# The sample's gathered rows of layer 0, issued without waiting for the first gate span

## The chip, the cores and the metric

The kernel runs on one core of one Trainium2 chip. The metric is the device time of one execution in microseconds (us). Engines are named as in the profile: PE is TensorE (PEld its weight loads), DVE is VectorE, ACT is ScalarE, POOL is GpSimd, SP is SyncE, whose queue issues the plain loads and stores.

## What is computed

One inference step of a two-layer encoder for two groups that share all weights: a prompt of 512 frames (four blocks of 128, B0 to B3) and a sample S of 64 frames. Each layer mixes (attention, mLSTM, chunk MLP) and then adds an expert layer:

```python
def layer(x, ...):
    x = x + concat([o_da, o_ml, o_cm]) @ w_out
    xn2 = rmsnorm(x, norm2_g)
    x = x + peer(xn2, peer_wq, peer_keys, peer_u, peer_v)

def peer(x, w_q, keys, u_tab, v_tab):            # per frame
    s = q(x) . keys                              # 8 heads, two halves of 128 keys
    e, g = top 16 of the 256 sums of two top-16 lists, softmax of their scores
    act = gelu(u_tab[e] . x)                     # 8 x 16 rows of 1024 of 16384
    return sum((g * act) * v_tab[e])
```

## The kernel before

The expert layer is done in two ways. For two blocks of each layer it is dense: all 16384 experts are multiplied on PE in 128 chunks, and a gate matrix W, zero except at the chosen experts, weights them. In layer 0 these are B0 and B1, in layer 1 B2 and B3. For the other two blocks and S only the chosen rows are fetched (gathered). A gather is one indirect DMA of POOL that fetches one row of 1024 float32 for each of 128 partitions (512 KB).

`gather_u` (L971) prepares the normalized frames: a sum of squares on ACT that uses the tile `xn` for its junk output (L236), a chain of small DVE operations for the inverse root (L226 to L231), and the scaled `xn` on DVE (L976). Then, for each of `npair` columns (128, for S 64, because S puts four heads on each half of the partitions), it gathers a row of `peer_u` (L960) and takes its dot product with `xn` on DVE (L984, and an accumulator read behind it). After each 32 of them ACT takes the GELU of 32 values (L987), and DVE multiplies them by the softmax weights (L988). `gather_v` (L992) gathers the rows of `peer_v` and adds each, times its factor, to x on DVE (L996). For S two small DMAs on the SP queue belong to it: L978 copies `xn` to the upper 64 partitions, and L1001 brings the upper half sum back. Rows come into six buffers (`row` 4, `row2` 2), and there is one `xn`.

One layer runs as a list of steps. For layer 0 the order is `N1 P1 N2 Q1 M1+P2 O1+Q2 S1+M2 F1+O2 S2`: N, P and Q are norm and projections, M the mixing, O the output projection (L396), S the scores and the top-16 selection (PE at L407 and L830, DVE at L912 to L953), F the end of the selection. Group 1 is B0, B1 and S; group 2 is B2 and B3. The selection of S is done early, inside S1, in two halves of 32 columns (the indices are written at L904). Then comes the first gate span (`first_gate`, 32 batches: DVE at L1020 to L1024, PE at L1028, ACT at L1030), woven with the first 12 chunks of the dense part (L1058), and the dense part itself (PE at L1058 and L1098, gate products on DVE at L1091, gelu on ACT at L1067). In layer 1 the order is `N1 P1 Q1 M1+R O1 S1 N2 P2 F1+Q2 M2 O2`, then S2 and the dense part; R is B3's `peer_v` rows of layer 0, spread over M1.

All instructions of an engine run in an order that is fixed when the program is built. A list scheduler goes through a model of time: whenever an engine is free in it, it takes the ready instruction with the most urgent priority. `low` (L1004) gives the gathers a very late priority, so that they are taken only when nothing else of that engine is ready, but an instruction once started is not broken off. `behind` adds an order to this without a semaphore: the later instruction must stand behind the earlier one on its engine. In layer 0 `gather_u` is called with `after=self.gated`, the last DVE instruction of the first gate span, so that the `xn` of each gathered group, and with it all its dot products, stands behind that span. In layer 1 there is no such order. The gathers of layer 0 go in the order S, B2, B3; B3's `peer_v` rows follow in layer 1 as R.

Of the kernel before, what the change touches and what calls it, by code (L numbers as in the profile page):

```python
# [92 lines left out]
def weave(*streams):  # L93
    live = [[g, n, 0] for g, n in streams]
    while live:
        r = min(live, key=lambda r: r[2] / r[1])
        r[2] += 1
        try:
            next(r[0])
        except StopIteration:  # L100
            live.remove(r)


def run(gen):
    for _ in gen:
        pass
# [14 lines left out]
class Build:  # L121
# [994 lines left out]
    def run(self):  # L1116
        tc = self.tc
        self.S = Tok("s", NS, None)
        self.B = [Tok(f"b{i}", P, i) for i in range(4)]
        self.setup()  # L1120
        S, B = self.S, self.B
        g1, g2 = [B[0], B[1], S], [B[2], B[3]]
        for t in [S] + B:
            t.npair = 64 if t.sample else P
            t.c0 = TD if t.sample else (t.blk % 2) * P
        for l in range(DEPTH):
            D = g2 if l else g1[:2]
            for i, t in enumerate([S] + B):
                t.dense, t.order, t.early = t in D, i, t.sample
            self.sel = self.ca.tile([P, TD // 8, 4, 8], F16, tag="sel", name="sel")  # L1130
            self.select_pool()
            with ExitStack() as es:
                self.mixer_pools(es.enter_context, l)
                L = self.layer_params(l)
                steps = {
                    "N1": lambda: [(self.norm_in(l, L, g1), 1)], "N2": lambda: [(self.norm_in(l, L, g2), 1)],
                    "P1": lambda: [(self.project_a(l, L, g1), 4)], "Q1": lambda: [(self.project_b(l, L, g1), 2)],
                    "P2": lambda: [(self.project_a(l, L, g2), 4)], "Q2": lambda: [(self.project_b(l, L, g2), 2)],
                    "M1": lambda: self.mix(l, L, g1), "M2": lambda: self.mix(l, L, g2),
                    "O1": lambda: [(self.out_proj(l, g1), 2)], "O2": lambda: [(self.out_proj(l, g2), 2)],  # L1140
                    "S1": lambda: [(self.scores(l, L, g1), 18)], "S2": lambda: [(self.scores(l, L, g2), 18)], "F1": lambda: [(self.finish_select(l, g1), 3)],
                    "R": lambda: [(self.rest_v(B[3], REST_STEP), REST_PARTS)]}
                for part in ORDER[l].split():
                    weave(*[s for k in part.split("+") for s in steps[k]()])
                if l == 0:
                    self.low(lambda: run(self.finish_select(l, g2)), by=MID)
            with ExitStack() as es:
                self.dense_pools(es.enter_context, l)
                nlead = LAG[l] + 8 * PRE[l]
                if l == 0:  # L1150
                    xT = self.split(self.dx.tile([P, KC, TD], F32, tag="xTd", name="xTd"))
                    self.norm_T(D, Q_G2, L, xT)
                    dense = self.peer_dense(l, D, xT)
                    weave((self.first_gate(l), 32), (itertools.islice(dense, nlead), nlead))
                else:
                    sc = self.scores(l, L, g2)
                    next(sc)
                    dense = self.peer_dense(l, D, self.xT2)
                    weave((itertools.islice(dense, EARLY_LEADS), EARLY_LEADS), (sc, 18))
                    run(itertools.islice(dense, nlead - EARLY_LEADS))  # L1160
                    run(self.finish_select(l, g2))
                    self.close_scores(es.enter_context, l)
                    run(self.first_gate(l))
                run(dense)
            for t in [S] + B:
                if not t.dense:
                    self.low(self.gather_u, l, L, t, None if l else self.gated)
                    if l or t is not B[3]:
                        self.low(self.gather_v, t, 0, P)
        self.fg = self.lp.tile([P, R_N], F32, tag="row", name="fg")[:, :DM]  # L1170
        self.nc.sync.dma_start(self.fg, self.bcast_rows(self.h["final_g"], DM))
        for t in [S] + B:
            self.final(t)
# [91 lines left out]
```

## Time and profile before

| quantity | value |
|---|---|
| median of 3 runs | 3612.36 us (3599.8 to 3621.32) |
| profiled execution | 3629.34 us, span 3627.6 us |
| PE busy | 3095.5 us (85%) |
| DVE busy | 2563.4 us (71%) |
| POOL busy | 1565.4 us (43%) |
| ACT busy | 670.5 us (18%) |
| DMA | 1060.20 MB, mean 292 GB/s |

Busy time is a sum over the whole span, whose stages have different limits, so stages are read one by one: the table by windows gives for each stretch the time for which each engine was busy, the TensorE clock that was granted (as a share of full speed), and the share and rate of the 16 DMA engines.

### The profile page before, as it was taken

The numbers are of one execution on the slowest core, as the hardware profiler recorded it, in microseconds if no ns is written. First come the engines' busy times: TensorE is split into PE (matmuls) and PEld (weight loads), VectorE is DVE, ScalarE is ACT, GpSimd is POOL, SyncE is SP. The second block draws the span as 40 slices with busy tenths as digits, with TensorE's granted clock in tenths as the row PEclk, the third lists the DMA queues.
The fourth block names the chain that finished last, engine by engine and source line by source line (L and its number), as shares of the span: only waits on it lengthen the run. The fifth ranks groups of instructions, "written<-read, shape, count | busy, mean of one in ns | idle before, by whom it ended". The sixth has DMA issues, their size and how long they took to land.

```text
span 3627.6 us, 41388 instructions
## 1 busy us (share of the span) xinstructions
PE 3095.5 (85%) x13384; PEld 2076.9 (57%) x13384; DVE 2563.4 (71%) x5915; ACT 670.5 (18%) x2589; POOL 1565.4 (43%) x1284
## 2 busy tenths in 40 slices
PE   8989877789999999985977896567566999999998
PEld 6767646646666666652543654245453566666655
DVE  4554677776687666666688898879998768766611
ACT  4444222400121000001222222111131002100000
POOL 0000000076545445455557335655667665666600
PEclk9999989899999999997978997688877999999999
DMA  5332322299999999998879687999888999999954
GB/s 180 100 101 76 98 90 82 85 354 403 374 343 398 409 407 407 409 396 324 327 216 351 238 317 278 288 335 332 323 303 293 408 407 361 382 402 400 398 172 122
DMA packets 299928, 1060.20 MB, mean 292 GB/s; under 512 B 36372, under 2 KB 39232, under 8 KB 299712
## 3 DMA queue, kind: packets, MB, share of 16 engines
q0 software_dynamic: 184320, 671.17, 49.7%
q1 hardware_dynamic: 115392, 386.38, 29.7%
q8 instruction: 107, 1.75, 0.2%
q14 instruction: 109, 0.89, 0.1%
HBM read 1048.09 MB, written 8.27 MB: 291 GB/s over the span
## 4 chain that ended last, share of the span: by engine, by line
PE 42%; DVE 17%; DMA 16%; issue 13%; POOL 7%; another core or an unknown queue 2%; ACT 2%; SPq 0%; POOLq 0%; DVEq 0%; ACTq 0%
PE y L1098 12%; PE H L1058 11%; DMA row<-in_peer_v_dram,idx 9%; POOL row L960 7%; PE ps L396 7%; PE ps L407 5%; DVE row L984 5%; DMA row<-in_peer_u_dram,idx 3%; DVE x_b L996 2%; DMA V<-in_peer_v_dram 2%; PE ps L572 1%; PE ps L1028 1%; PE ps L574 1%; DVE i L913 1%
## 5 line engine op out<-in xcount | busy, mean ns | idle before, releaser
L960 POOL DMA_INDIRECT row<-in_peer_u_dram,idx x640 | 773.2, 1208 | 1358.1 <-DVE row L984 670.4
L960 POOL DMA_INDIRECT row<-in_peer_v_dram,idx x640 | 792.0, 1238 | 522.4 <-DVE x_b L996 262.2
L984 DVE SCALAR_TENSOR_TENSOR row<-row,xn 128x1024 f32<-128x1024 f32 x640 | 773.1, 1222 | 156.1 <-DMA row<-in_peer_u_dram,idx 149.4
L1098 PE MATMUL y<-V,A 128*128 128x512 f32 x1856 | 835.1, 598 | 25.4 <-DMA V<-in_peer_v_dram 18.0
L996 DVE SCALAR_TENSOR_TENSOR x_b<-row,hb,x_b 128x1024 f32<-128x1024 f32 x512 | 656.4, 1282 | 148.8 <-DMA row<-in_peer_v_dram,idx 138.3
L1098 PEld LDWEIGHTS y<-V,A 128*128 128x128 f32 x1856 | 352.5, 192 | 403.0 <-issue 371.9
L1058 PE MATMUL H<-xT,U 128*128 128x256 f32 x2048 | 485.6, 391 | 55.3 <-ACT pre L1067 24.4
L1058 PE MATMUL H<-xTd,U 128*128 128x256 f32 x2048 | 470.1, 383 | 12.0 <-ACT A L1067 10.0
L1058 PEld LDWEIGHTS H<-xT,U 128*128 128x128 f32 x2048 | 393.6, 195 | 149.4 <-issue 35.0
L1058 PEld LDWEIGHTS H<-xTd,U 128*128 128x128 f32 x2048 | 388.0, 191 | 105.8 <-issue 41.0
L407 PE MATMUL ps<-xT,w 128*128 128x320 f32 (+1 forms) x1280 | 343.4, 424 | 33.6 <-DMA w<-in_wt_dram 22.5
L1067 ACT ACTIVATE A<-H 128x256 f32<-128x256 f32 x232 | 89.1, 384 | 1388.2 <-PE H L1058 770.6
L1091 DVE TENSOR_TENSOR A<-A,W 128x256 f32<-128x256 f32 x232 | 97.1, 423 | 333.7 <-ACT A L1067 330.1
L407 PEld LDWEIGHTS ps<-xT,w 128*128 128x128 f32 x1280 | 248.8, 199 | 103.7 <-issue 15.1
L1030 ACT ACTIVATE W<-ps 128x64 f32<-128x64 f32 x1024 | 137.5, 321 | 260.7 <-PE ps L1028 151.9
L996 DVE SCALAR_TENSOR_TENSOR x_s<-row,hb,x_s 128x1024 f32<-128x1024 f32 x128 | 164.1, 1282 | 21.5 <-DMA row<-in_peer_v_dram,idx 19.5
L396 PE MATMUL ps<-w,xT 128*128 128x512 f32 (+3 forms) x320 | 133.1, 567 | 22.1 <-DMA w<-in_wn_dram 15.8
L1028 PE MATMUL ps<-o,o 128*128 128x64 f16 x2048 | 87.4, 200 | 73.9 <-DVE o L1024 73.7
L1028 PEld LDWEIGHTS <-o 128*128 128x128 f16 x2048 | 81.2, 103 | 106.5 <-issue 50.4
L1098 PE MATMUL y<-V,pre 128*128 128x512 f32 x192 | 100.6, 681 | 24.6 <-DMA V<-in_peer_v_dram 21.7
L351 DVE TENSOR_TENSOR wl<-w,wh 128x1024 fp32r<-128x1024 f32 (+1 forms) x56 | 64.4, 1150 | 76.3 <-PE ps L396 56.5
L1020 DVE TENSOR_TENSOR o<-jj,sel 128x1024 f16<-128x1024 f16 x128 | 87.9, 688 | 41.2 <-PE ps L1028 39.8
(314 smaller groups left out, 3049.3 us busy)
## 6 DMA issues: line engine op xcount, KB each, us to landing
V<-in_peer_v_dram SPq DMA_DIRECT2D x256, 512.0 KB
U<-in_uT_dram SPq DMA_DIRECT2D x256, 512.0 KB
w<-in_wt_dram SPq DMA_DIRECT2D x96, 512.0 KB
w<-in_wn_dram SPq DMA_DIRECT2D x80, 512.0 KB
row<-in_peer_u_dram,idx POOLq DMA_INDIRECT x640
row<-in_peer_v_dram,idx POOLq DMA_INDIRECT x640
w<-in_keysT_dram SPq DMA_DIRECT2D x16, 256.0 KB
w<-in_wn_dram SPq DMA_DIRECT2D x8, 264.0 KB
```

The costliest lines, as they stand in the source:

```text
L396: self.nc.tensor.matmul(p[:t.n, :wd], x[kk][:, t.c0:t.c0 + t.n], ww[:, k * wd:(k + 1) * wd], start=(kk + part + j == 0), stop=(kk == KC - ...
L407: self.nc.tensor.matmul(ps, ww[:, k * P:(k + 1) * P], x[k][:, :n], start=(k + part + j == 0), stop=(k == KC - 1 and part == pair and j == ...
L960: self.nc.gpsimd.indirect_dma_start(out=row, out_offset=None, in_=self.h[tab], in_offset=bass.IndirectOffsetOnAxis(ap=t.idx[:, k:k + 1], a ...
L984: nc.vector.scalar_tensor_tensor(row, row, 1.0, xn, op0=ALU.mult, op1=ALU.mult, accum_out=hb[:, k:k + 1])
L996: op = nc.vector.scalar_tensor_tensor(x, row, t.hb[:, k:k + 1], x, op0=ALU.mult, op1=ALU.add)
L1020: nc.vector.tensor_tensor(o2, self.jj[:, None].to_broadcast([P, 4, P, 2]), sel[:, 1, :, None, :].to_broadcast([P, 4, P, 2]), op=ALU.is_equal)
L1028: nc.tensor.matmul(pb[:, j, :nq], o2[:, j // 2, :, j % 2], o1[:, p, j // 2, :, j % 2], start=(p == 0), stop=(p == 1))
L1030: nc.scalar.activation(W[:, :, t0:t0 + 8].rearrange("p i t -> p t i"), pb[:, :, 8 * i:8 * i + 8], AF.Copy, scale=1.0 / GSCALE)
L1058: mm = nc.tensor.matmul(hp, U[:, k, :], xT[k], start=(k == 0), stop=(k == KC - 1))
L1067: nc.scalar.activation(a, hp, AF.Gelu)
L1091: gated = nc.vector.tensor_tensor(a, a, Ws[ci // 8][:, ci % 8, :], op=ALU.mult)
L1098: nc.tensor.matmul(ys[i][:, hf, :], a[:, i * P:(i + 1) * P], V[:, hf * 512:(hf + 1) * 512], start=(c == 0), stop=(c == NCH - 1))
```

## The change

The order behind the first gate span is left out for S in layer 0. B2 and B3 keep it. Nothing else is edited.

```diff
             for t in [S] + B:
                 if not t.dense:
-                    self.low(self.gather_u, l, L, t, None if l else self.gated)
+                    self.low(self.gather_u, l, L, t, None if l or t.sample else self.gated)
                     if l or t is not B[3]:
                         self.low(self.gather_v, t, 0, P)
```

## Rows read from the trace of the kernel before

**Rows 1.** Page, section 5: group of instructions, busy us, mean ns, idle before it.

```profile
L996 DVE SCALAR_TENSOR_TENSOR x_s<-row,hb,x_s 128x1024 f32<-128x1024 f32 x128 | 164.1, 1282 | 21.5 <-DMA row<-in_peer_v_dram,idx 19.5
```

**Rows 2.** Timeline of POOL: start, duration, instruction, idle time before and releaser.

```profile
408.77 1.07 POOL L960 DMA_INDIRECT row<-in_peer_u_dram,idx  x1 [408.31 <-DVE on L609]
...
731.09 6.27 POOL L960 DMA_INDIRECT row<-in_peer_u_dram,idx  x1 [315.03 <-DVE row L984]
```

**Rows 3.** Timeline of DVE: S's second indices, its scaled frames, its first dot product.

```profile
491.54 0.19 DVE L904 SCALAR_TENSOR_TENSOR idx<-es 128x32 int32<-128x32 f32 x1
...
720.63 1.27 DVE L976 SCALAR_TENSOR_TENSOR xn<-x_s,rs_y,row 64x1024 f32<-64x1024 f32 x1
...
729.60 1.21 DVE L984 SCALAR_TENSOR_TENSOR row<-row,xn 128x1024 f32<-128x1024 f32 x1
```

**Rows 4.** Windows of layer 0: stretch, length, busy us (instructions) by engine, clock, DMA.

```profile
core 0: us, PE busy (x) PEld busy (x) DVE busy (x) ACT busy (x) POOL busy (x), PEclk, DMA share, GB/s
408.00:490.00 82.00, 54.77 (x238) 36.86 (x236) 60.16 (x362) 19.74 (x76) 5.76 (x6) 0.83 0.38 110
490.00:522.00 32.00, 26.39 (x62) 11.89 (x62) 25.05 (x63) 6.74 (x16) 0.00 (x0) 0.87 0.39 123
522.00:612.00 90.00, 80.82 (x420) 71.40 (x421) 53.43 (x336) 21.89 (x84) 0.00 (x0) 0.95 0.30 91
612.00:648.00 36.00, 6.96 (x47) 6.26 (x46) 35.49 (x162) 4.86 (x18) 0.00 (x0) 0.65 0.05 15
648.00:722.00 74.00, 67.90 (x736) 59.88 (x735) 50.74 (x97) 38.34 (x266) 0.00 (x0) 0.94 0.35 101
```

**Rows 5.** The same windows for S2 and the end of selection in layer 1.

```profile
2407.00:2550.00 143.00, 105.85 (x498) 89.77 (x498) 128.53 (x467) 22.92 (x81) 83.50 (x72) 0.88 0.94 340
2550.00:2648.00 98.00, 56.90 (x202) 44.56 (x202) 94.51 (x269) 12.98 (x28) 66.07 (x51) 0.79 0.92 335
```

**Rows 6.** Windows of L984 alone (DVE): second stretch of rows 5.

```profile
2550.00:2648.00 98.00, 56.18 (x92) 0.79 0.92 335
```

**Rows 7.** Line L984 within 2407 to 2550: idle before it, and who waited for it.

```profile
  DMA row<-in_peer_u_dram,idx: 13.7, 10
...
  ACT hb L987: 36.2, 2
```

**Rows 8.** Line L830, idle of PE before it (us, times): 522 to 612, then 2407 to 2550.

```profile
  ACT pq L824: 5.8, 8
...
  ACT pq L824: 50.9, 18
```

**Rows 9.** Timeline of DVE in the end of selection in layer 1.

```profile
2626.65 1.21 DVE L984 SCALAR_TENSOR_TENSOR row<-row,xn 128x1024 f32<-128x1024 f32 x1
...
2627.79 0.28 DVE L894 TENSOR_TENSOR sel<-gr,sel 128x128 f16<-128x128 f32 x1
2628.00 1.21 DVE L984 SCALAR_TENSOR_TENSOR row<-row,xn 128x1024 f32<-128x1024 f32 x1
```

**Rows 10.** Windows of the dense part of layer 0, its end, and the start of layer 1.

```profile
729.00:1636.00 907.00, 863.59 (x3339) 555.28 (x3337) 636.73 (x928) 85.00 (x384) 498.51 (x436) 0.98 1.00 391
1550.00:1600.00 50.00, 47.51 (x163) 31.23 (x163) 33.40 (x65) 5.30 (x10) 28.17 (x25) 0.97 1.01 396
1600.00:1636.00 36.00, 26.75 (x65) 12.50 (x63) 24.72 (x43) 0.77 (x2) 21.30 (x19) 0.91 1.01 393
1636.00:1706.00 70.00, 28.29 (x86) 14.95 (x86) 57.12 (x110) 11.02 (x34) 50.52 (x46) 0.70 0.98 365
1706.00:1794.00 88.00, 86.20 (x249) 42.05 (x248) 40.75 (x84) 16.26 (x34) 42.05 (x30) 0.97 0.77 279
```

**Rows 11.** Timelines at the start of layer 1: DVE's root chain (first and last), PE.

```profile
1646.97 0.17 DVE L226 TENSOR_SCALAR rs_v<-ssn 128x3 f32<-128x3 f32 x1
...
1656.67 0.16 DVE L231 SCALAR_TENSOR_TENSOR rs_y<-rs_t,rs_y 128x3 f32<-128x3 f32 x1
...
1705.29 10.46 PE L396 MATMUL ps<-w,xT 128*128 128x512 f32 x16 [14.47 <-DMA w<-in_wn_dram]
```

## The prediction

> **What bounds the kernel now.** I read the table by windows first, because the change moves work between stages with different limits. In the dense part of layer 0, 729 to 1636 us, PE is busy 863.6 of 907 us while the DMA share is 1.00 and DVE is busy only 636.7 us [rows 10]. The reader is to see that PE sets the end there, and that 436 gathers are served beside it at almost no cost. In the mixer that goes before, 408 to 722 us, the DMA share is 0.05 to 0.39 [rows 4]: this is where the change puts the sample's gathers. But DVE is far from idle: 21.8 + 7.0 + 36.6 + 0.5 + 23.3 = 89.2 us are free in 314. Who sets the pace changes from stretch to stretch. In 522 to 612 (the scores) PE is busy 80.8 of 90 us; in 612 to 648 (the end of the selection) DVE is busy 35.5 of 36 and PE 7.0.
>
> The timelines of POOL and DVE come next. Six gathers of the sample are issued from 408.8 us on, as many as there are row buffers; the next one waits 315.0 us for a dot product [rows 2]. The scaled frames come at 720.6 us among the last operations of the gate span, and the first dot product at 729.6 [rows 3]. So the order that the change removes does bind. Without it the sample's first 32 columns can run from about 410 us, the other 32 from 491.5, when their indices are written [rows 3], then the 64 of `peer_v`.
>
> **What moves.** The sample has 64 dot products and 64 additions. A dot product costs DVE 1.22 us (56.18 us for 46 with their accumulator reads [rows 6]), an addition 1.28 [rows 1]: 78 + 82 = 160 us of DVE, and 122 gathers of 512 KB (six are early already). One scaling (1.27 us [rows 3]), two small GELUs on ACT, and the two SP copies L978 and L1001 move with them. POOL carries nothing but gathers, so nothing queues behind them there. On SP weight loads stand behind the two copies, and on ACT the evacuations of PE's results stand behind the GELUs; that is in the cost below.
>
> **What it costs before the gate.** If all 128 are done before the gate span ends, DVE needs 160 us and has 89.2: at least 71 us longer, if DVE binds. If only idle time is filled, 0. No reason allows less than 0, as work is only added there. The nearest rows are the same stages in layer 1, which run with gathers at the same late priority and without the order.
>
> First, 408 to 490: 32 dot products, 39 us, against 21.8 free; between 0 and 17, I take 10.
>
> Second, 490 to 612: in layer 1, 72 gathers were issued in the 143 us of the scores [rows 5], 0.5 per us. By that rate about 66 fit in these 122 us and the time that they add. PE's idle time in the scores grew from 9.2 us (90 - 80.8 [rows 4]) to 37.2 (143 - 105.9 [rows 5]), thus 28 us or 0.39 us per gather. How it comes is in the rows: ACT's GELU of the factors waited 36.2 us for dot products [rows 7], and PE waited 50.9 us for ACT's evacuation, against 5.8 in layer 0 [rows 8]. 13.7 us of DVE's waits there were for rows under a DMA share of 0.94 [rows 5, 7], which the mixer of layer 0 does not have. So 0.2 to 0.39 each, 13 to 26 us; I take 20.
>
> Third, 612 to 648: the remaining 30. Here the pattern is plain. In layer 1 a dot product stands between almost every two selection operations [rows 9], since the later one is not ready at the moment at which the earlier one ends in the scheduler's model, and a late priority loses only to what is ready. DVE's own work in that stage is about equal in both layers (94.5 - 56.2 = 38 us with a few additions in it; 35.5 in layer 0), yet it took 98 us with 51 gathers and 36 without [rows 4 to 6]: 1.2 us each. 30 x 1.2 = 36 us, between 0 and 36.
>
> The gate span of 74 us is then left with no sample work: 0. Sum: 10 + 20 + 36 = 66 us, bounds 0 and 95. The upper one is 17 + 26 + 36, and 16 for the copies on SP and the GELU's waits, which a mean from layer 1 may miss.
>
> **What it gives back.** The dense part then starts on B2 at once. B2 and B3 have 128 + 128 + 128 gathers left, against 436 served before [rows 10], so B3's `peer_u` rows end some 50 gathers before the dense part does, and the 76 that now run in 1636 to 1794 (46 and 30 [rows 10]) are gone. That B3's `peer_v` rows could use the room is excluded: they are tied to M1 of layer 1. The gains are three. The end of the dense part: PE lost 2.5 us in 1550 to 1600 and 9.2 in 1600 to 1636 [rows 10]; I take 9 of 11.7. The start of layer 1: 70 us in 1636 to 1706 with PE busy 28.3, at 0.70 of the clock, because the root chain took 9.9 us with dot products between its small steps and PE then waited 14.5 us for a weight load under a DMA share of 0.98 [rows 10, 11]. The chain alone is 11 steps of under 0.2 us, so 7.6 us are sure; with the load and the low clock I take 25, at most 42 (70 - 28.3). The rest to 1794: PE is busy 86.2 of 88, so at most 1.8, taken as 2. Sum: 36 us, bounds 15 and 55.
>
> A page speaks for more. The Trainium skill, Perfetto Trace Analysis, section Optimization Strategy, says that a kernel whose most-contended engine changes over time may gain by interleaving the regimes. The DMA shares of 0.3 and 1.00 look like such a pair; what it would give here is the first rival. The trace agrees only in part, since the engine with slack in the dense part is DVE, and DVE is what the selection lacks.
>
> **Forecast.** 66 - 36 = +30 us. Against the profile's own execution of 3629.34 that is 3659; it lies 17 us above the median of 3612.36, so the median to expect is 3642 us.
>
> **Rivals.**
> First, faster: the list scheduler puts sample rows only where DVE is idle. Then 89.2 / 1.25 = 71 columns move, nearly the 76 that layer 1 gets rid of, and the rest stays behind the gate. Cost about 5, gain 36: -31, 3581 us. It decides in 612 to 648: if under 5 sample rows stand among the selection, this is what happened. For it: PE sets the pace in 490 to 612, where DVE has 43.6 us free [rows 4]. Against it: the dense row of insertions in layer 1 [rows 9].
> Second, no change: the insertions cost about what the start of layer 1 gives back, for example 10 instead of 30 in the end of the selection (66 - 24 = 42 against 36): +6, 3618 us. Here belongs also that the change does nothing, because something else holds the sample's scaled frames; against that, x of the sample is final after O1, before the scores that gave the indices of the gathers at 408.8 us [rows 2], so that only the order is left.
> Third, worse: each GELU holds ACT as long as in layer 1 (36.2 us for two [rows 7]) and PE with it, and DVE has no free slot: 95 against 25: +70, 3682 us.
>
> **How the numbers follow.** The forecast has a chance of 0.40, the first rival 0.20, the second 0.27, the third 0.13. A measurement of this kernel can tell about 0.5%, 18 us, from no change. So faster 0.20, same 0.27, slower 0.53. For 8 in 10 the range reaches half into the first and the third rival: 3583 to 3682 us. The forecast's own range is 3625 to 3665.
>
> **What the profile would show.** POOL issues the sample's gathers through 410 to 720 us and not from 731; DVE is over 90% busy from 490 to the end of the selection; the gate span (L1028) begins at about 714 instead of 648 us [rows 4]; B3's last dot product stands before the end of the dense part; and the stretch from that end to the first full-speed projection shrinks from 70 to about 45 us. I am wrong in the sign if L1028 comes less than 36 us late, and wrong in the mechanism if DVE shows free time among the selection while the stage is still longer.

## The result, and the profile after

The changed kernel took 3669.82 us (median of four runs, 3662.56 to 3676.45), the kernel before 3616.84 beside it: a ratio of 1.0172, 95% interval 1.0147 to 1.0197, or 53 us more. In a second series, with both kernels run again, it was 3675.81 against 3612.67, 1.0193 (1.0154 to 1.0233). The forecast was 3642 us, 30 more than the median then known.

The stages tell where it went. Each number is the start, in us, of the first or last instruction of a line; the two columns "again" are the profiles of the second series.

| boundary | before | after | before, again | after, again |
|---|---|---|---|---|
| first score product, L830 | 310.6 | 315.2 | 314.7 | 312.9 |
| S's second indices, L904 | 491.5 | 514.6 | 493.8 | 512.2 |
| last score product, L831 | 610.8 | 675.1 | 618.4 | 678.3 |
| first gate product, L1028 | 649.4 | 747.8 | 657.0 | 745.3 |
| end of the dense part, first of the last two L1105 | 1639.7 | 1724.3 | 1648.4 | 1722.4 |
| last first projection of layer 1, L396 | 1769.8 | 1817.3 | 1757.5 | 1816.2 |
| last L1105 | 3612.0 | 3655.2 | 3597.9 | 3658.7 |

From the first score product to the first gate product the kernel before took 338.8 and 342.3 us, the changed one 432.6 and 432.4. Six further kernels below leave this stage as it was before (335 to 341 us), and one that leaves the sample out has 334.2; I call 338 us the stage without sample rows, and the cost is then **94 us**. From there to the last L1105 the changed kernel took 2907.4 and 2913.4 us against 2962.6 and 2940.9: it gets 55 us back by the first pair of profiles and 27.5 by the second. Leaving the sample out gives 32 us in run times (below), so the second pair is nearer to the typical case.

Windows of the profile after, over the stretches of [rows 4] as they now lie (length, busy us and instructions by engine, clock, DMA share, GB/s):

```profile
core 0: us, PE busy (x) PEld busy (x) DVE busy (x) ACT busy (x) POOL busy (x), PEclk, DMA share, GB/s
408.00:490.00 82.00, 51.83 (x222) 34.24 (x223) 76.12 (x301) 17.17 (x63) 38.58 (x32) 0.86 0.76 264
490.00:522.00 32.00, 16.84 (x44) 9.61 (x43) 29.61 (x167) 6.88 (x19) 5.72 (x5) 0.56 0.23 76
522.00:612.00 90.00, 61.79 (x231) 42.24 (x230) 83.36 (x214) 19.30 (x60) 58.37 (x47) 0.83 0.95 354
612.00:680.00 68.00, 55.56 (x274) 47.28 (x273) 67.96 (x240) 14.16 (x55) 36.05 (x33) 0.90 0.91 323
680.00:747.00 67.00, 2.60 (x13) 2.04 (x12) 66.37 (x233) 3.69 (x8) 19.09 (x19) 0.54 0.48 152
```

DVE, busy 60.2 of the first 82 us and 53.4 of the 90 us of the scores before [rows 4], is now full from 408 us to the gate: 323.4 of 339 us. PE no longer sets the pace; in 522 to 612 it is busy 61.8 us instead of 80.8. The DMA share, 0.30 among the scores before, is 0.95.

POOL's timeline shows the sample's gathers where [rows 2] had the wait of 315 us (start, duration, instruction, idle before and releaser). The first gather of the first 32 columns, the first and the last of the other 96, and the first row of B2 stand here:

```profile
413.33 1.08 POOL L960 DMA_INDIRECT row<-in_peer_u_dram,idx  x1 [412.88 <-DVE on L609]
...
515.06 1.68 POOL L960 DMA_INDIRECT row<-in_peer_u_dram,idx  x1 [38.91 <-DVE idx L904]
...
707.38 0.94 POOL L960 DMA_INDIRECT row<-in_peer_v_dram,idx  x1 [1.99 <-DVE cand L914]
737.78 1.68 POOL L960 DMA_INDIRECT row<-in_peer_u_dram,idx  x1 [29.46 <-DVE idx L904]
```

DVE's timeline in the end of the selection has the picture that [rows 9] showed for layer 1, an addition of 1.26 us among operations of 0.1 to 0.3:

```profile
691.49 0.27 DVE L913 FIND_INDEX8 i<-v,s 128x8 uint32<-128x128 f32 x1
691.69 1.25 DVE L996 SCALAR_TENSOR_TENSOR x_s<-row,hb,x_s 128x1024 f32<-128x1024 f32 x1
692.88 0.07 DVE L916 MATCH_VALUE_LOAD ci<-vsel,cand 128x8 f32 x1
...
694.34 0.26 DVE L914 MATCH_REPLACE8 s<-v,s 128x128 f32<-128x128 f32 x1
694.53 1.26 DVE L996 SCALAR_TENSOR_TENSOR x_s<-row,hb,x_s 128x1024 f32<-128x1024 f32 x1
695.72 0.07 DVE L914 MATCH_VALUE_LOAD s<-v,s 128x8 f32 x1
```

Who kept PE waiting between 408 us and the gate, after (engine, line and releaser: us in total, times, longest):

```profile
PE ps L754 <- DVE kn L748: 23.4, 1, 23.4
PE ps L407 <- DMA w<-in_wt_dram: 17.1, 8, 5.6
PE ps L884 <- DVE es L953: 12.6, 2, 10.0
PE ps L214 <- DVE oh L952: 11.3, 1, 11.3
PE ps L830 <- ACT pq L824: 6.1, 10, 1.4
```

The three large single waits, 23.4, 10.0 and 11.3 us, are for DVE: mixing and selection that come late behind sample rows. Waits for weights (`in_wt`) come next, 17.1 us against 7.6 from 408 us to the gate of the kernel before. The wait for a score's evacuation, 50.9 us in layer 1 [rows 8] and the mechanism of the third rival, is 6.1 us.

At the other end B3's last dot product (the last start in the first line, L984) now stands 101 us ahead of the end of the dense part. Where [rows 11] had 9.9 us, the root chain at the start of layer 1 takes 2 us, and full-speed projections begin 20 us after the dense end:

```profile
L984 DVE SCALAR_TENSOR_TENSOR row<-row,xn x128: 1212/1220/1276, 1357.5 to 1622.8; 128x1024 f32<-128x1024 f32 x128
...
1724.30 1.23 DVE L1105 TENSOR_TENSOR x_b<-y,x_b 128x1024 f32<-128x1024 f32 x1 [4.31 <-PE y L1098]
1729.70 0.17 DVE L226 TENSOR_SCALAR rs_v<-ssn 128x3 f32<-128x3 f32 x1 [2.03 <-ACT junk L367]
1731.67 0.16 DVE L231 SCALAR_TENSOR_TENSOR rs_y<-rs_t,rs_y 128x3 f32<-128x3 f32 x1
1744.24 18.98 PE L396 MATMUL ps<-w,xT 128*128 128x512 f32 x42
```

### The profile page after: what moved, and what is told of

It reads as the page before. It is cut to its first block, busy times and chain, and to the rows that moved or that the text cites. A ratio compares the mean times of both kernels' runs of the same rounds, so it can differ in the third digit from the quotient of the medians.

```text
span 3670.8 us, 41380 instructions
## 1 busy us (share of the span) xinstructions
PE 3092.7 (84%) x13384; PEld 2066.4 (56%) x13384; DVE 2539.6 (69%) x5915; ACT 675.5 (18%) x2593; POOL 1614.5 (44%) x1284
## 4 chain that ended last, share of the span: by engine, by line
PE 57%; DVE 21%; issue 10%; DMA 8%; ACT 2%; POOL 2%; SPq 0%; DVEq 0%; POOLq 0%; ACTq 0%
PE y L1098 21%; PE H L1058 19%; PE ps L396 7%; DVE row L984 5%; PE ps L407 3%; DMA row<-in_peer_v_dram,idx 3%; DMA row<-in_peer_u_dram,idx 2%; DVE x_b L996 2%; DMA V<-in_peer_v_dram 2%; DVE x_s L996 2%; POOL row L960 2%; PE ps L1028 1%; PE ps L572 1%; ACT A L1067 1%; DVE i L913 1%
## 5 line engine op out<-in xcount | busy, mean ns | idle before, releaser
L960 POOL DMA_INDIRECT row<-in_peer_u_dram,idx x640 | 781.1, 1221 | 1152.4 <-DVE on L609 412.9
L960 POOL DMA_INDIRECT row<-in_peer_v_dram,idx x640 | 833.2, 1302 | 713.9 <-DVE x_b L996 441.8
L984 DVE SCALAR_TENSOR_TENSOR row<-row,xn 128x1024 f32<-128x1024 f32 x640 | 768.0, 1221 | 91.6 <-DMA row<-in_peer_u_dram,idx 87.4
L1098 PE MATMUL y<-V,A 128*128 128x512 f32 x1856 | 824.3, 595 | 5.3 <-DMA V<-in_peer_v_dram 5.3
L996 DVE SCALAR_TENSOR_TENSOR x_b<-row,hb,x_b 128x1024 f32<-128x1024 f32 x512 | 655.7, 1281 | 69.1 <-DMA row<-in_peer_v_dram,idx 56.9
L1098 PEld LDWEIGHTS y<-V,A 128*128 128x128 f32 x1856 | 352.3, 191 | 393.3 <-issue 380.0
L1091 DVE TENSOR_TENSOR A<-A,W 128x256 f32<-128x256 f32 x232 | 97.2, 424 | 551.8 <-ACT A L1067 551.3
L407 PE MATMUL ps<-xT,w 128*128 128x320 f32 (+1 forms) x1280 | 347.6, 428 | 41.7 <-DMA w<-in_wt_dram 39.3
L407 PEld LDWEIGHTS ps<-xT,w 128*128 128x128 f32 x1280 | 251.5, 201 | 113.8 <-DMA w<-in_wt_dram 38.2
L1028 PE MATMUL ps<-o,o 128*128 128x64 f16 x2048 | 85.7, 201 | 109.7 <-DVE o L1024 109.0
L996 DVE SCALAR_TENSOR_TENSOR x_s<-row,hb,x_s 128x1024 f32<-128x1024 f32 x128 | 163.1, 1274 | 14.0 <-DMA row<-in_peer_v_dram,idx 13.2
L1028 PEld LDWEIGHTS <-o 128*128 128x128 f16 x2048 | 79.8, 103 | 139.2 <-issue 77.1
L396 PE MATMUL ps<-w,xT 128*128 128x512 f32 (+3 forms) x320 | 128.7, 553 | 10.5 <-ACT v L448 7.1
L1098 PE MATMUL y<-V,pre 128*128 128x512 f32 x192 | 101.2, 683 | 34.7 <-DMA V<-in_peer_v_dram 29.5
L396 PE MATMUL ps<-w,mix 128*128 128x512 f32 (+1 forms) x224 | 115.7, 672 | 8.5 <-DMA w<-in_wn_dram 7.0
```

What stands on the lines that cost most here:

```text
L396: self.nc.tensor.matmul(p[:t.n, :wd], x[kk][:, t.c0:t.c0 + t.n], ww[:, k * wd:(k + 1) * wd], start=(kk + part + j == 0), stop=(kk == KC - ...
L407: self.nc.tensor.matmul(ps, ww[:, k * P:(k + 1) * P], x[k][:, :n], start=(k + part + j == 0), stop=(k == KC - 1 and part == pair and j == ...
L960: self.nc.gpsimd.indirect_dma_start(out=row, out_offset=None, in_=self.h[tab], in_offset=bass.IndirectOffsetOnAxis(ap=t.idx[:, k:k + 1], a ...
L984: nc.vector.scalar_tensor_tensor(row, row, 1.0, xn, op0=ALU.mult, op1=ALU.mult, accum_out=hb[:, k:k + 1])
L996: op = nc.vector.scalar_tensor_tensor(x, row, t.hb[:, k:k + 1], x, op0=ALU.mult, op1=ALU.add)
L1028: nc.tensor.matmul(pb[:, j, :nq], o2[:, j // 2, :, j % 2], o1[:, p, j // 2, :, j % 2], start=(p == 0), stop=(p == 1))
```

## The experiments

Two questions: what the 94 us consist of, and what a row costs by the place at which it stands. Times are medians with the ratio to the kernel before in the same series; "gate" is the time from the first score product to the first gate product, to be held against 338 us.

**Both kernels again.** No edit.

> The kernel before, unchanged, on the chip of these experiments, to lay its stages beside theirs: its profiled execution so far came from another series and lay above the median. Leaving out the sample's rows gave 32 us in time, while the two profiles differ by 65 us from the first gate product to the end. Expected: median about 3602 us, and from L1028 to the end about 2930 us instead of 2963; if it is 2963 again, the medians and the profiles contradict each other.

3610.54 us; from L1028 to the end 2940.9 us in the profile, near the 2930 expected. The kernel before lost 130 us between L1105 and the last first projection in its first profile and 109 in this one (granted clock 0.89 and 0.98 in the 107 and 86 us after the first of those projections), so that first profile held an unusually slow start of layer 1.

> The changed kernel, unchanged, in the same series: about 3602 x 1.0172 = 3664 us. With it the cost is 3664 - 3570 = 94 us against the kernel without the sample's rows, and what the dense part and the start of layer 1 give back is 3602 - 3570 = 32 us. If the forecast's cost of 66 us were right, it would come to 3636 us.

3675.81 us, 63 more than the kernel before in this series; a cost of 66 us would have given 34 more. The cost is not 66.

**No sample rows in layer 0.**

```
-                if not t.dense:
+                if not t.dense and (l or not t.sample):
                     self.low(self.gather_u, ...
```

> Leaves out all of the sample's expert rows in layer 0 (64 gathers of peer_u, 64 of peer_v, their dot products and additions), so the time is that of a kernel with less work. It prices both sides of the change at once. Theory (DVE work): the trace of the changed kernel puts the first gate product (L1028) 98 us later than before and gives 59 us back in the dense part and in layer 1. Then this kernel has the mixer of the kernel before (L1028 at about 650 us) and the dense part of the changed one: about 3670 - 100 = 3570 us. Rival (the price of the forecast, 66 us, was right and something else was lost later): about 3604 us.

3569.62 us, ratio 0.992 (0.9893 to 0.9948); gate 334.2. So in the kernel before the sample's rows cost 32 us, nearly all after the gate, and that is about the most that the change could have brought. By the ratios the changed kernel, 1.0172 and 1.0193, stands 91 to 98 us above this one, which is the cost ahead of the gate.

**Narrow rows.** The gathers stay, DVE's share of them goes.

```
-  scalar_tensor_tensor(row, row, 1.0, xn, ...)
+  w = 32 if t.sample and not l else DM
+  scalar_tensor_tensor(row[:, :w], row[:, :w], 1.0, xn[:, :w], ...)      # likewise L996
```

> The changed kernel, but in layer 0 the sample's dot products and additions go over 32 of the 1024 columns of a row; all 128 gathers, both GELUs, the copies and the order stay. The result of those rows is therefore only partly computed. Theory (the added DVE time is the cost): 160 us of DVE shrink to some 15 to 25, so L1028 starts under 670 us instead of 748 and the time is 3575 to 3590 us. Rival (waits in order: the GELUs in front of ACT's evacuations, the copies and the gathers' traffic against the weight loads): most of the cost stays, L1028 at 715 us or later, time 3635 us or more.

3627.15 us, 1.0075 (1.0054 to 1.0096); gate 386.0. Neither: half of the cost stays, though the row operations take DVE 27.9 us, accumulator reads included, instead of 160. The waits of DVE from 408 us to the gate say why; the changed kernel's own, in the second series, stand in the last line:

```profile
DVE x_s L999 <- DMA row<-in_peer_v_dram,idx: 39.9, 31, 2.8
DVE row L986 <- DMA row<-in_peer_u_dram,idx: 31.8, 24, 4.8
...
DVE row L984 <- DMA row<-in_peer_u_dram,idx: 10.8, 7, 4.7
```

With short row operations DVE comes to each row before it has landed and waits, 71.7 us in all, and the selection behind it waits too. The Trainium skill, "DVE: scalar operands, raw-bit mode, write accounting and state across instructions", section "Flops that outlive an instruction", says that DVE's queue is one in-order queue; this trace agrees. In the changed kernel the rows' arrival is mostly hidden behind DVE's own work, and 10.8 to 13.6 us of waiting are left.

**The same work without the gathers**, free and then confined to the window of the changed kernel.

```
-  row = self.gather(t, "peer_u", k)
+  src = xn if t.sample and not l else self.gather(...)       # a row that lies in SBUF
...
+  self.behind(op, self.ix[k // 32])        # second kernel only: behind L904 of each half
```

> The changed kernel, but the sample's rows of layer 0 are not gathered: the dot products and additions go at full width over a row that already lies in SBUF. It leaves out 128 gathers of 512 KB and computes other values. Theory (DVE work): the cost stays, L1028 at 735 us or later, time 3655 to 3675 us. Rival (the gathers' traffic holds up weight loads; the DMA share is 0.95 in the changed kernel's scores): L1028 under 700 us, time under 3625 us.

3654.08 us, 1.0146; gate 393.1, outside both. Without indices to wait for, the dot products began at 303 us and used idle time that the changed kernel can't reach, so this did not decide. Its time is not used either: the dense part of layer 1 ran slower in it (last section).

> The changed kernel with the sample's rows of layer 0 not gathered (the dot products and additions go over a row that already lies in SBUF; other values are computed), but each half of the dot products still ordered behind the operation that writes its indices (L904), so that all of DVE's 160 us fall into the same window as in the changed kernel, which they did not when they were free from 290 us on. Theory (DVE's time alone: 160 us less the 66 us that DVE had free): L1028 comes 80 to 98 us later than before, as in the changed kernel. Rival (the wait for the row in DVE's order is a cost of its own that adds to it, 47 us as in the kernel with narrow rows): the DVE part is then 98 - 47 = 51 us, L1028 at about 700 us.

3663.57 us in a single run; gate 417.7, 80 us longer. DVE's time alone gives 80 of the 94, though here no row stood behind the last score product (the last one started at 668 us). The remaining 14 come with the gathers (one profile of each; the stage repeated within 4 us in the kernel before). DVE's waits for rows are about as long, but PE's waits for weights (L407) also differ, 21.4 us in the changed kernel again and 5.8 here; no run tells the two apart. Windows from the first sample row to the first gate product: the kernel before again, the changed kernel again, this kernel, and the one with narrow rows.

```profile
413.00:657.00 244.00, 172.81 (x763) 129.10 (x762) 174.95 (x920) 52.66 (x191) 5.67 (x6) 0.83 0.29 89
...
411.00:745.00 334.00, 179.65 (x761) 131.12 (x760) 318.80 (x1126) 59.91 (x199) 156.31 (x134) 0.77 0.74 264
...
411.00:731.00 320.00, 173.00 (x763) 127.64 (x762) 316.38 (x1129) 59.48 (x201) 6.40 (x6) 0.77 0.23 66
...
408.00:696.00 288.00, 175.86 (x763) 128.31 (x762) 197.44 (x1128) 60.02 (x201) 130.72 (x134) 0.80 0.82 306
```

The third busy number is DVE: 175 us without the rows, 319 and 316 with them, thus 141 to 144 more (under the 160 of the forecast, since neighbouring operations overlap by some 0.06 us: above, the addition of 691.69 us ends at 692.94 and the next operation starts at 692.88). Idle time fell from 69 us to 15 and 4. That is the account: 144 of work, 54 of it in idle time, 90 on the path.

**Half of the rows.** The dot products free, the additions behind the gate span; then only the first 32 dot products free.

```
-  self.low(self.gather_v, t, 0, P)
+  self.low(self.gather_v, t, 0, P, self.gated.ins if t.sample and not l else None)
...
+  self.behind(op, self.gated.ins)        # second kernel: dot products 32 to 63
```

> Only the first half of the change: the sample's 64 dot products of layer 0 are free to run early, its 64 additions stay behind the first gate span. Theory (DVE work): 64 dot products are 78 us of DVE against 66 us that DVE had free from 408 to 648 us, of which the changed kernel filled 50; so L1028 comes 12 to 40 us later than before. 64 gathers less remain for the dense part, of the 76 that ran after it before, which keeps most of the 59 us that came back, 40 to 50. Time about 3617 + 26 - 45 = 3598 us, between 3580 and 3620. Rival (the waits that the GELUs bring): all of them come with the dot products, so L1028 comes 60 us later or more and the time is 3630 us or more.

3618.64 us, 1.0039 (1.0022 to 1.0056); gate 382.9, 45 us for 64 rows. A little over the expected 12 to 40 us; 28 us come back in the time.

> The sample's first 32 dot products of layer 0 are free, the other 32 and the additions stay behind the gate span. Theory (they run from 409 to 490 us, in front of the mixing and selecting chains of DVE): the second list of indices comes 19 us later, as it did with all 64 free, the scores after it can't win that back, and L1028 comes 15 to 20 us later; 32 rows fewer at the end give about 13: 3602 + 18 - 13 = 3607 us. Rival (the scores are bound by PE and take up what DVE is late): L1028 under 8 us later, time about 3594 us.

3634.39 us, 1.0092 (1.0063 to 1.012); gate 360.6, 23 us for 32 rows. PE-bound scores don't win the delay back. The time is worse than expected: the 13 us that should have come back did not (see Open, below).

**Rows placed in the idle time of the scores**, and some in the gate span.

```
+  self.bunch += [self.last_dve()]        # after the norm and after each group of selected heads
...
+  self.behind(op, self.bunch[k // 7 * 2] if k < 28 else self.gated.ins)
+  # second kernel, k >= 28: self.marks[min(2 * (k - 28) + 1, 31)], every second gate batch
```

> 28 of the sample's 64 dot products of layer 0 stand ahead of the gate span, and each is ordered behind a point of the scores of B2 and B3 (L841): seven behind the norm, seven behind each of the first three groups of selected heads. The other 36 and the additions stay behind the gate span as before. In the kernel before PE sets the pace there and DVE has 36.6 us free between 522 and 612 us, 29 rows' worth. Theory (a row costs only where it stands in front of work that others wait for): the last score matmul and L1028 come at most 8 us later than before. 28 rows fewer remain of the 76 that ran after the dense part; leaving out all 128 gave 32 us, so these give about 12. Time 3602 + 5 - 12 = 3595 us. Rival (a row costs 0.7 to 0.8 us wherever it stands, as the second 32 dot products did: 44 - 19 = 25 us): L1028 some 21 us later, time about 3611 us.

3624.25 us, 1.0057 (1.0037 to 1.0077); gate 351.9, 14 us for 28 rows. Paced rows cost 0.5 us each, less than free ones and far from nothing, though DVE kept 17.7 us free in 522 to 612. They ran in four blocks of seven, each 8 us long; rows spread one by one were not tried. And again nothing of 12 us came back.

> As the kernel with 28 paced rows, and 15 further dot products are let into the first gate span, one behind every second batch of eight tokens. In the kernel before DVE waits 1.32 us for PE in front of every second batch there, and a row takes 1.22 us and 0.08. Theory: the gate span grows by under 4 us and 43 rows are gone from the end, worth about 18 us: 3602 + 7 - 18 = 3591 us. Rival (the batch's one-hot tiles come later by each row, since PE is fed with no reserve): 15 us longer, time about 3603 us or more.

3654.44 us, 1.0137 (1.0111 to 1.0163); gate 357.7, and from there to the first L1098 82.3 us. The kernel before takes 74.8 for that span, but the kernel with 28 paced rows alone takes 81.7 (see Open), so the 15 rows in it cost under 1 us there. By stages 27 us are lost, where the theory had 7; the other half of the 52 lies in layer 1, where the time from the last first projection to the last L1105 was 1868.6 us, 28 more than in the kernel before again (last section).

| kernel | rows ahead of the gate | longer than 338 us | us per row |
|---|---|---|---|
| paced | 28 | 14 (20 with rows in the gate span) | 0.5 to 0.7 |
| first 32 dot products | 32 | 23 | 0.7 |
| all dot products | 64 | 45 | 0.7 |
| changed kernel | 128 | 94 | 0.73 |
| not gathered, same window | 128 | 80 | 0.62 |
| gathered, narrow | 128 | 48 | 0.37 |

So up to the gate the price of free rows is about even, 0.7 us: DVE's 1.2 us less the share that falls into idle time, and a part for the gathers' traffic. Stage by stage it is not even, because work that is late in one stage is paid for in the next (below).

**The opposite in layer 1.** The forecast had taken its rates from layer 1, where this order doesn't exist. If a row ahead of the gate is dear there too, holding some back should help. All these kernels are the kernel before with one or two ties more.

```
-  self.low(self.gather_u, l, L, t, None if l else self.gated)
+  self.low(self.gather_u, l, L, t, None if l and t.sample else self.gated)       # B0, B1 held
...
+  self.behind(op, self.gated.ins)        # B0's dot products from the 17th, 41st or 57th on
+  self.low(self.gather_v, t, k0, P, self.selend)       # S's additions from k0 = 0 or 32 on
```

B0 and B1 held, and S's additions from the first on:

> The kernel before (layer 0 untouched), and in layer 1 the opposite of the change: the sample's dot products stay free, its additions wait for the end of the selection and the rows of B0 and B1 for the end of the first gate span. In the kernel before 51 gathers stood among the selection of layer 1 (2550 to 2648 us, 98 us, where layer 0 without them took 36), and the gathers ended at 3455 us of a dense part that ended at 3612. Theory (rows among the selection cost their full time, rows beside the dense part nothing): the gate span of layer 1 starts some 50 to 60 us earlier against the start of its scores, and the time is 3602 - 55 = 3547 us. Rival (the dense part of layer 1 can't take 59 rows more and they run out past its end, or the selection is long for another reason): 3590 us or more.

B0 and B1 held, and S's additions from the 33rd on:

> The kernel before with half of the hold in layer 1: the sample's dot products and its first 32 additions are free, its last 32 additions wait for the end of the selection, and the rows of B0 and B1 for the end of the first gate span. With all 64 additions held the dense part ended 128 us sooner (3484 us against 3612), but the gathers ran on for 170 us behind it; in the kernel before they ended 157 us ahead of it. Theory (both ends move evenly with the rows held, so that they meet near the middle): dense end and last gather near 3550 us, time about 3545 us. Rival (the gathers of the dense part can't be served faster than before, whichever rows they are, so nearly every held row is added behind its end): over 3590 us.

Only B0 and B1 held:

> The kernel before with the order that the change removes added where it was missing: in layer 1 the rows of B0 and B1 wait for the end of the first gate span, the sample's 128 rows stay free. In the kernel before some 81 rows of B0 run ahead of that gate and 38 in it. Theory (a row ahead of the gate costs DVE's time or more, a row beside the dense part nothing as long as the gathers end first): holding 113 rows moved the dense end from 3598 to 3510 us and the last row from 3441 to 3602; by the row that is 0.78 and 1.4 us, so 81 rows give a dense end near 3535 and a last row near 3556: time about 3570 us, 1.0 to 1.5% faster than before. Rival (what the dense part of layer 1 can serve is fixed, so that each held row is added at the end; the kernel with 113 held rows was no faster): 3600 us or more.

B0's first 16, 40 and 56 dot products free:

> As the kernel that holds B0 and B1 in layer 1, but the first 16 dot products of B0 stay free: some 65 rows held. By the same rates the dense part ends near 3547 us and the last row near 3533, so PE sets the end again: about 3562 us. Rival: 3600 us or more; or, if a row ahead of the gate costs only the 0.39 us that the forecast took from the scores of layer 1, both kernels gain less than 30 us.

> The kernel before with the rows of B0 from the 41st on, and those of B1, held behind the first gate span of layer 1. With 16 free rows the gate came 80 us earlier, the dense part ended at 3506 us and the last row at 3569. Theory (the rows in between cost 1.2 us each ahead of the gate, and 1.3 to 1.5 us each at the end of the gathers): dense end near 3535 us, last row near 3535, time about 3555 us, 1.5% faster than before. Rival (the price isn't row by row; the order in which the scheduler lays the whole stage out decides): the gate stays within 10 us of 2552 or falls back to 2631, and the time is then about 3540 or 3600 us.

> The same with 56 free rows of B0. Theory: gate 20 us later than with 40, dense end near 3555 us, last row near 3515, time about 3573 us. Rival: as for the kernel with 40 free rows, the gate at either end (2552 or 2631).

The gate at 2552 us in the last two texts is a misreading, the edge of the stretch that was read and not the first product; their rival rests on it and falls. The text on B0 and B1 counts 81 rows ahead of the gate; the trace has 132. None of the six times came out as the theory had it. With 16 rows free and with none both kernels gained less than 30 us, as the rival with the price of 0.39 us says, but not for its reason: the gate came 106 and 126 us earlier, and the other end took it back. The first gate products of layer 1 stand in the table, from the first score product of layer 1 on:

| kernel | rows fewer ahead of the gate | gate | us won per row | dense end | last row | time, ratio |
|---|---|---|---|---|---|---|
| before, again | 0 | 654.5 | | 3597.9 | 3440.9 | 3610.5 |
| 56 free | 76 | 563.7 | 1.2 | 3516.3 | 3520.1 | 3547.6, 0.9844 |
| 40 free | 92 | 550.2 | 1.1 | 3500.5 | 3528.3 | 3568.6, 0.9899 |
| 16 free | 116 | 548.6 | 0.9 | 3505.8 | 3568.6 | 3594.4, 0.9958 |
| B0, B1 held | 132 | 528.9 | 0.95 | 3511.0 | 3596.5 | 3635.9, 1.0085 |
| and 32 additions | 160 | 515.5 | 0.9 | 3509.7 | 3601.9 | 3622.1, 1.0024 |
| and 64 additions | 192 | 485.7 | 0.9 | 3483.9 | 3630.0 | 3649.7, 1.012 |

Of the 132 rows of B0 and B1, 55 had stood behind the last score product; without them that stretch fell from 110.6 to 42.7 us, 1.2 us each. The other 77 stood among the scores; from the last L396 ahead of them to the last score product the kernel before again and then the one with B0 and B1 held took 157.2 and 107.7 us, 0.64 us for each row:

```profile
2363.60:2520.80 157.20, 102.44 (x497) 87.21 (x496) 137.32 (x474) 27.85 (x94) 86.14 (x76) 0.84 0.89 326
...
2343.50:2451.20 107.70, 95.78 (x497) 83.41 (x496) 55.42 (x354) 27.67 (x92) 0.00 (x0) 0.97 0.36 116
```

Held rows come out of the other end: the last row moves from 157 us ahead of the dense end to 146 behind it, and where it is well behind, gathers set the time. That is what the rivals of the first three texts expected of their kernels. (B0 and B1 held alone is slower than with 32 additions more because its dense part ran slower, last section.) With 56 free rows both ends meet, and this kernel beats both others: 3547.61 us, 0.9844 (0.9811 to 0.9877). Windows of the scores, the end of the selection and the gate span of layer 1 in the kernel before again, and then of the scores and the end of the selection in this one:

```profile
2400.00:2521.00 121.00, 88.24 (x427) 74.92 (x425) 110.45 (x415) 17.51 (x66) 66.94 (x60) 0.87 0.93 346
2521.00:2631.00 110.00, 64.92 (x230) 51.20 (x230) 105.99 (x311) 13.69 (x31) 75.42 (x56) 0.78 0.91 329
2631.00:2730.00 99.00, 58.36 (x660) 49.31 (x659) 96.49 (x145) 36.84 (x264) 65.84 (x39) 0.74 0.76 261
...
2400.00:2492.00 92.00, 78.96 (x390) 67.45 (x389) 87.65 (x399) 15.89 (x60) 42.53 (x36) 0.94 0.83 314
2492.00:2534.00 42.00, 37.09 (x164) 29.92 (x164) 38.04 (x163) 10.73 (x23) 0.00 (x0) 1.00 0.40 126
```

The end of the selection shrinks from 110 to 42 us without POOL's 56 gathers: 1.2 us for each.

## Why the prediction was right and wrong

**Sign and mechanism** held: the sample's rows fill DVE ahead of the gate; DVE is over 90% busy from 490 us to the end of the selection (0.93, 0.93, 1.00 and 0.99 in the windows), and the gate comes late by more than what layer 1 gives back. The time, 3669.8, lies in the range of 3583 to 3682, which reached that far only to take in half of the third rival, and outside the forecast's own of 3625 to 3665.

**The cost before the gate was mis-sized**: 66 us forecast, 94 and some 3 in the gate span measured. Term by term, from the first and the second pair of profiles (the stages end at L904, the last score product and the first gate product, wherever they lie):

| term | forecast (bounds) | measured |
|---|---|---|
| 408 to 490, first 32 rows | 10 (0 to 17) | 18 and 20 |
| 490 to 612, 66 rows (77 and 79 in the traces) | 20 (13 to 26) | 41 and 41 |
| 612 to 648, the rest, 30 (19 and 17) | 36 (0 to 36) | 34 and 28 |
| gate span, to the first L1098 | 0 | 3 and 3 |
| gain, dense part from the first L1098 | 9 | 17 and 17 |
| gain, start of layer 1 | 25 (7.6 to 42) | 37 and 15 |
| gain, rest | 2 | 4 and -2 |

The step that failed is the second term, and its method. It priced a gather among the scores by PE's idle time in layer 1, 0.2 to 0.39 us [rows 5], took 0.3, and left the wait for rows out because the mixer of layer 0 does not have a DMA share of 0.94. Windows of the scores, before and after, and of the end of the selection, before, after, and after for the additions alone (L996, DVE):

```profile
491.50:610.80 119.30, 105.47 (x474) 82.00 (x474) 75.78 (x387) 27.95 (x97) 0.00 (x0) 0.94 0.33 102
514.60:675.10 160.50, 119.07 (x477) 87.56 (x476) 151.53 (x441) 30.09 (x99) 95.91 (x81) 0.84 0.93 340
...
610.80:649.40 38.60, 7.65 (x52) 6.87 (x52) 38.09 (x168) 5.31 (x20) 0.00 (x0) 0.65 0.05 14
675.10:747.80 72.70, 7.55 (x54) 6.85 (x53) 72.07 (x255) 7.75 (x23) 23.32 (x21) 0.57 0.48 151
675.10:747.80 72.70, 25.17 (x20) 0.57 0.48 151
```

PE's idle time grew from 13.8 to 41.4 us, which is 0.36 for each of the 77 rows and inside the forecast's rate. But PE's busy time grew too, by 13.6 us for about the same matmuls, at a granted clock of 0.84 instead of 0.94, the mean of each stretch; the forecast had no term for that. In the second pair the two parts are 35 us (0.45 a row) and 6. The DMA share that was to be missing came along with the gathers, 0.93, with 10.8 to 13.6 us of DVE's waits for rows before the gate. At its source the rate was low too: taking the rows out of the scores of layer 1 gave 0.64 us each. The first term, 18 and 20 us for 10, came out a little over its upper bound of 17, which holds if all of DVE's idle time is used; 6 of the 22 us stayed idle.

The forecast had also passed a floor of its own. It said that with all rows ahead of the gate DVE needs at least 71 us more, and then added stretch prices to 66. The floor was itself too low, since it counted the gate span's 23.3 idle us, which no sample row reached: POOL's last one was issued at 707 us and the gate began at 748. Without them it is 160 - 65.9 = 94 us, the measured cost; that it is met so exactly is partly chance, as DVE's net work was 144, 15 us stayed idle and 11 of these were waits for rows.

**The third term** has the right pattern, but its size is met by luck. Only 19 and 17 rows stood there, not 30: by the windows above 25 us of DVE (22 in the second pair). The other 9 (6) of the 34 (28) us are DVE's own work that had come late from the scores, 47 us instead of 38. The price of 1.2 us per row itself held, also in layer 1, where each row taken out of the end of the selection gave that much.

**The gain** was about right: 36 forecast, 30 by the second pair of profiles, 58 by the first (27.5 and 55 from the first gate product on, where the gate span's 3 are taken off). Its causes are as forecast, no gathers left after the dense part and a root chain of 2 us; its parts are not, 17 for 9 in the dense part and 15 for 25 at the start of layer 1 in the second pair. What differs between the pairs is the kernel before, whose first profile started layer 1 20 us slower. The stretch from the dense end to full-speed projections shrank to 20 us, not 45, and in the kernel before again it had been 46, not 70.

**The rivals.** Faster, by idle time alone, is out: 54 us of idle were used, and the rest did not stay behind the gate. It decided at five rows among the selection; 19 of the 64 additions (17 in the second series) started after the last score product. No change is out too, at 1.7 and 1.9% with intervals that start at 1.5. The third had nearly the size, 95 - 25 = 70, but not its mechanism: ACT's GELUs did wait for dot products, 19.8 us, but PE waited 6.1 us for evacuations, not 50.9. What it had right is that DVE has hardly any free time left, 15 us.

**The page** that spoke for the change, the Trainium skill's Perfetto Trace Analysis, section Optimization Strategy, says that interleaving stages with different most-contended engines may help. DMA was evened out (0.29 to 0.74 ahead of the gate) and the time grew, because the moved rows also need DVE, the engine that this stage lacks. With 56 free rows in layer 1 a move did pay: there rows went from the DVE-bound stage to the one with DVE to spare.

**Open:** why 28 to 32 early rows gave nothing back in the time, where 64 gave 28 us and all 128 at most 32. The traces of these kernels show two parts of it. Six dot products whose rows had already landed stand in one block ahead of the last gate batch (743.9 to 750.8 us with 32 free rows); PE's first L1098 waits 8.3 us there for DVE's gate products (L1091), 2.7 in the kernel before again, and the gate span to the first L1098 takes 81.5 and 81.7 us instead of 74.9. The dense part then gives back 5 to 7 us, about as much. And the start of layer 1 still has gathers in it: 110.7 and 107.8 us from the dense end to the last first projection, against 109.1. The rest is not explained.

## What to carry to other kernels

Before pricing a move stretch by stretch, add up the moved work on each engine over the whole stretch up to the next fixed point, and take off only the idle time that the work can reach: that is a floor for the cost, and no sum of local prices may fall below it. A late priority does not make work free: on an in-order engine it goes wherever nothing else is ready at that moment and then delays what becomes ready next, here by 0.5 to 1.2 us for operations of 1.2. A price taken from idle time alone leaves out that the other engine's own work can take longer, here PE's matmuls by 6 to 14 us. Look for the point at which both ends meet, the last deferred row and the end of the bound stage; here it was worth 1.6%.

## What the hardware showed beyond that

Shorter work on DVE did not remove the cost of waiting in order: with the row operations cut to a 32nd, DVE still lost 72 us to rows that had not landed, at a DMA share of 0.82 and 306 GB/s.

The dense part of layer 1 ran at two speeds for the same instructions. In the window from 3200 to 3400 us of the kernel with only B0 and B1 held, the one with rows in the gate span, and the one with free rows that were not gathered, the DMA engines moved 378 to 381 GB/s and PE was busy 93.8%; in the other kernels it was 398 to 407 GB/s (371 without the sample's rows, where fewer gathers ran) and 96.7% or more. Both kinds, B0 and B1 held and then 16 rows free:

```profile
3200.00:3400.00 200.00, 187.68 (x630) 117.36 (x629) 120.23 (x218) 11.69 (x31) 118.75 (x93) 1.00 0.99 378
...
3200.00:3400.00 200.00, 193.37 (x663) 124.47 (x662) 130.13 (x221) 13.49 (x35) 131.95 (x97) 1.00 1.02 399
```

Over the 700 us of this stage that would be some 20 us, an estimate from this window; it is most of the 25 that the kernel with rows in the gate span lost beyond its stages in layer 0. What sets the speed was not found.
